# Larger load packets and smaller store packets for two of twelve slabs of a rotation kernel, and an earlier first store

## Chip, cores, metric

One core of a Trainium2 chip. The metric is the device time of one execution in microseconds (us). The kernel is bound by its DMA transfers from the second microsecond to the last.

## The reference

```python
def setup_inputs():
    batch, c, h, w = 32, 3, 256, 256
    return {"x": np.random.randn(batch, c, h, w).astype(np.float32)}

def reference(x):
    return np.rot90(x, k=-1, axes=(-2, -1)).astype(np.float32)
```

96 images of 256 x 256 floats are turned by 90 degrees: 25.17 MB in, 25.17 MB out.

## The kernel before

Twelve slabs of 8 images lie in SBUF (2.1 MB each; 4096 floats per partition). A slab comes in one of two layouts. In the *short* layout a partition holds 8 rows of each of two images, and the HBM side is runs of 8 KB; in the *long* layout it holds 16 rows of one image, runs of 16 KB. The turn on the vector engine changes one layout into the other: what is loaded short is stored long, and what is loaded long is stored short. (The two pairs 8, 9 and 10, 11 are long on both sides.) One run becomes one DMA packet, so the layout decides the packet size of the load and, the other way round, of the store.

```python
    RL, RS = 16, 8
    I = 2
    ...
    long_st = (0, 1, 2)            # loaded short, stored long
    both = (8, 10)
    ...
    for n in (0, 1, 2, 3, 7, 4, 5, 6, *range(8, n_slabs)):
        if n in (1, 2):
            nc.sync.dma_start(out=fours(units[n]), in_=ld_short[n])          # 2 MB, 8 KB packets
            continue
        for i in range(I):
            if n in long_st:
                ld = nc.sync.dma_start(out=fours(units[n])[:, i], in_=ld_short[n][:, i])
            else:
                ld = nc.sync.dma_start(out=units[n][i::I], in_=ld_long[n, i])  # 1 MB, 16 KB packets
            if (n, i) == (last, 0):
                mark = ld
    ...
    def store(n):
        if n in paired:
            first = n if n in both else n - 1
            for i in range(I):
                nc.sync.dma_start(out=st_long[n, i], in_=pairs[both.index(first)][n - first :: I, i])
        elif n in long_st:
            for i in range(I):
                nc.sync.dma_start(out=st_long[n, i], in_=home[n][i::I])
        else:
            return nc.sync.dma_start(out=st_short[n], in_=fours(home[n]))   # 2 MB, 8 KB packets

    for n in range(both[0]):
        turn(n)
    for n in (4, 3, 5, 6, 7, 1, 2):
        st = store(n)
        if n == 4:
            # the first store waits for the load called mark
            tc.add_manual_dep(st.ins, mark.ins.name, ...)
    for n in range(both[0], n_slabs):
        turn(n)
        store(n)
    ...                                # the copies of slab 0, then store(0)
```

All transfers are issued by one queue, at most eight are outstanding. Loads come first, then five stores of 8 KB packets (slabs 4, 3, 5, 6, 7), then stores of 16 KB packets.

## Time and profile before

| | |
|---|---|
| device time, median (range) of the first 3 runs | 123.25 us (123.25 to 123.33) |
| span of the profiled execution | 121.5 us |
| DMA share of the span | 97.9% |
| vector engine busy | 90.6 us (75%) |
| transfers: loads | 20 of 1 MB, 2 of 2 MB |
| transfers: stores | 14 of 1 MB, 5 of 2 MB |

The span is shorter than the device time by a constant 1.8 us or so. The lines that carry the reading are shown in the prediction. Two things help to follow the rest. A *landing* is the moment when a transfer's completion arrives; each of the 16 DMA engines reports its own, so a landing has a middle (median engine) and an end (slowest engine). And the trace records each packet with start, size and duration, but not its engine, and each engine's arrival of a completion; where I say "packet records" or "arrivals" I mean these.

### The profile page before, as it was taken

To read this page: it belongs to the slowest core of one execution; us is meant where nothing else is said; L and a number is where in the kernel's file an instruction comes from. 1 tells how busy PE (TensorE), PEld (TensorE's weight loads), DVE (VectorE), ACT (ScalarE), POOL (GpSimd) and SP (SyncE) were. 2 spreads that over 40 slices of the span, in tenths; PEclk is the share of its full clock that TensorE was granted. 3 is DMA by queue.
4 is the path that set the end of the run, shared out by engine and by line. 5 is a ranking of instruction groups with operands and counts; after the bars stand their busy time and mean duration, and the time that the engine had idled before them with its cause. 6 is when DMAs were issued, how large, how long until landed. Compare 5 with 4: busy or idle time off the path is not lost.

```text
span 121.5 us, 134 instructions
## 1 busy us (share of the span) xinstructions
DVE 90.6 (75%) x24; ACT 4.9 (4%) x3; POOL 0.2 (0%) x4
## 2 busy tenths in 40 slices
DVE  0029999999999999999999999999999960000000
ACT  0000000000000000000040000000000038000000
POOL 0000000000000000000000000000000000000000
DMA  3999999999999999999999999999999999999994
GB/s 73 426 429 426 432 458 426 426 421 421 432 432 432 421 432 432 426 426 432 432 405 426 421 429 431 432 423 431 453 432 432 432 432 432 432 432 432 432 432 173
DMA packets 4752, 50.33 MB, mean 414 GB/s; under 512 B 656, under 2 KB 656, under 8 KB 656
## 3 DMA queue, kind: packets, MB, share of 16 engines
q1 hardware_dynamic: 4752, 50.33, 97.9%
HBM read 25.17 MB, written 25.17 MB: 414 GB/s over the span
## 4 chain that ended last, share of the span: by engine, by line
DVE 59%; issue 13%; DMA 6%; DVEq 3%; ACT 2%; ACTq 1%; SPq 0%
DVE u L116 53%; DVE turned L116 6%; DMA u<-in_x_dram 6%; DVEq L169 3%; ACT u L141 2%; ACTq L169 1%; SPq L92 0%; DVEq L116 0%
## 5 line engine op out<-in xcount | busy, mean ns | idle before, releaser
L116 DVE STREAM_TRANSPOSE u<-u 128x2048 f32<-128x2048 f32 x22 | 83.5, 3866 | 0.3
L116 DVE STREAM_TRANSPOSE turned<-u 128x2048 f32<-128x2048 f32 x2 | 7.1, 3586 | 8.2 <-DMA u<-in_x_dram 8.2
L141 ACT COPY u<-turned 128x2048 f32<-128x2048 f32 x2 | 3.6, 1869 | 35.6 <-DVE u L116 35.6
L141 ACT ACT_TABLE_LOAD x1 | 1.3, 1283 | 62.2 <-DMA u<-in_x_dram 62.2
L158 POOL MEMSET const-bfloat16-1.0<- 128x1 bf16 x1 | 0.1, 101 | 0.0
L158 POOL MEMSET const-uint8-127<- 128x1 uint8 x1 | 0.1, 101 | 0.0
L158 POOL MEMSET const-float32-0.0<- 128x1 f32 x1 | 0.1, 98 | 0.2 <-issue 0.2
L158 POOL MEMSET const-float32-1.0<- 128x1 f32 x1 | 0.1, 98 | 0.0
## 6 DMA issues: line engine op xcount, KB each, us to landing
u<-in_x_dram SPq DMA_DIRECT2D x20, 1024.0 KB, 19.6
out_dram<-u SPq DMA_DIRECT2D x14, 1024.0 KB, 15.6
out_dram<-u SPq DMA_DIRECT2D x5, 2048.0 KB, 16.0
u<-in_x_dram SPq DMA_DIRECT2D x2, 2048.0 KB, 13.7
```

The source lines that it names most:

```text
L116: nc.vector.transpose(out=dst[:, h * step : (h + 1) * step], in_=src[:, h * step : (h + 1) * step])
L141: nc.scalar.copy(out=fours(units[last])[:, i], in_=fours(turned0)[:, i])
L158: nc = _bacc.Bacc("TRN2", target_bir_lowering=False, num_devices=1)
L169: with _tile.TileContext(nc) as tc:
```

## The change

Its intent: slabs 1 and 2 change layout, so that their loads use 16 KB packets, which were cheaper while loading, and their stores the 8 KB form. The last slab's first load is cut into 14 rows and 2 rows, and the first store waits for the 14 rows only. The diff also merges the two stores of slabs 8 and 10 into one transfer each.

```diff
-    long_st = (0, 1, 2)
+    long_st = (0,)
@@
-        if n in (1, 2):
+        if n in ():
             nc.sync.dma_start(out=fours(units[n]), in_=ld_short[n])
             continue
@@ the long loads
-                ld = nc.sync.dma_start(out=units[n][i::I], in_=ld_long[n, i])
-            if (n, i) == (last, 0):
-                mark = ld
+                cuts = (0, 14 * W, RL * W) if (n, i) == (last, 0) else (0, RL * W)
+                for f0, f1 in zip(cuts, cuts[1:]):
+                    ld = nc.sync.dma_start(out=units[n][i::I, f0:f1], in_=ld_long[n, i][:, f0:f1])
+                    if f1 == 14 * W:
+                        mark = ld
@@ def store(n):
         if n in paired:
             first = n if n in both else n - 1
+            if n == first:
+                nc.sync.dma_start(out=st_long[n].transpose([1, 0, 2]), in_=pairs[both.index(n)][::I])
+                return
```

## The prediction

> **What bounds the kernel now.** I read the page from the top. Slices first: is any engine, or the DMA row, full throughout?
>
> ```profile
> DVE  0029999999999999999999999999999960000000
> DMA  3999999999999999999999999999999999999994
> GB/s 73 426 429 426 432 458 426 426 421 421 432 432 432 421 432 432 426 426 432 432 405 426 421 429 431 432 423 431 453 432 432 432 432 432 432 432 432 432 432 173
> DMA packets 4752, 50.33 MB, mean 414 GB/s; under 512 B 656, under 2 KB 656, under 8 KB 656
> q1 hardware_dynamic: 4752, 50.33, 97.9%
> ```
>
> The DMA row is 9 from the second slice to the last but one, and its share of the span is 97.9%. The vector engine (DVE) is full for two thirds, then stops with 22 us to go. 50.33 MB is input plus output, so no byte can be saved: the time is a short start, one unbroken stream on 16 engines, and a short tail. 656 small packets are 41 transfers by 16 engines; the other 4096 carry data, half of 16 KB and half of 8 KB.
>
> One slice says 405, two say 458 and 453. A packet is counted whole where it starts, so I asked for the stages apart, with borders inside stretches of one kind, and for two windows of equal length around the turn from loads to stores:
>
> ```profile
> core 0: us, DVE busy (x) ACT busy (x) POOL busy (x), PEclk, DMA share, GB/s
> 20.50:59.70 39.20, 39.03 (x11) 0.00 (x0) 0.00 (x0) 1.00 1.01 429
> 66.60:86.10 19.50, 19.43 (x6) 0.00 (x0) 0.00 (x0) 1.00 1.01 429
> 88.60:118.00 29.40, 10.54 (x3) 3.63 (x2) 0.00 (x0) 1.00 1.01 429
> ...
> 54.00:59.00 5.00, 4.97 (x3) 0.00 (x0) 0.00 (x0) 1.00 1.02 433
> 59.00:64.00 5.00, 4.97 (x2) 1.28 (x1) 0.00 (x0) 1.00 0.97 411
> ```
>
> Loads of 16 KB, stores of 8 KB and stores of 16 KB run at the same 429. The window of the turn shows 0.97. Is that a real hole of 0.15 us, or counting? At its left edge 16 KB packets (0.614 us) that began earlier are lost, half a packet on average, 0.31 us; at its right edge 8 KB packets (0.310 us) give back only 0.155. The difference, 0.15 us of 5, is the 3% that is missing. A second reading confirms it: the first store is issued at 59.77 (timeline) and lands 7.3 us later, at 67.07 (the shortest of its line's landings, third row below); the scalar engine's table load, which waits for a load, is let go at 62.24, so the last load has landed by then.
>
> ```profile
> 59.77 3.29 SPq L127 DMA_DIRECT2D out_dram<-u  x4
> 62.24 1.28 ACT L141 ACT_TABLE_LOAD   x1 [62.24 <-DMA u<-in_x_dram]
> DMA to landing us min/median/max: 7.3/16.0/19.2
> ```
>
> From 62.24 to 67.07 are 4.83 us, and 2.10 MB at 429 GB/s need 4.89. There is no room for a hole. I also laid the trace's packet records side by side: the first begins at 1.77 us, the last ends at 120.30, and from 3.0 to 120.0 the 16 engines are never short of a packet. Durations of single packets and arrivals on single engines below are from these records too.
>
> **What a load of either form costs.** Eight transfers may be outstanding, so in the load stage each issue is released by the landing of the one eight earlier. The issue times are landings. The timeline of the queue, asked in narrow windows:
>
> ```profile
> 8.14 0.47 SPq L94 DMA_DIRECT2D u<-in_x_dram  x1
> 13.12 0.47 SPq L94 DMA_DIRECT2D u<-in_x_dram  x1
> 18.09 0.47 SPq L94 DMA_DIRECT2D u<-in_x_dram  x1
> ...
> 20.53 0.47 SPq L94 DMA_DIRECT2D u<-in_x_dram  x1
> 30.32 0.47 SPq L94 DMA_DIRECT2D u<-in_x_dram  x1
> ```
>
> 8.14 to 18.09 is the passage of slabs 1 and 2 in 8 KB packets: 9.95 us. 20.53 to 30.32 is four 16 KB transfers of 1 MB, the same 4.19 MB: 9.79 us.
>
> **What the Trainium skill says.** In "DMA: Bandwidth & Descriptors", section "Why small descriptors are slow (HBM only)", each packet carries a fixed overhead of about 3 cycles and 32 bytes of metadata. The trace agrees in kind: load packets average 310.0 ns for 8 KB and 614.1 ns for 16 KB, so two small ones cost 5.9 ns more than a large one, about 1%. The same page, section "Queues, rings and completion order", says that each engine consumes descriptors in ring order; so a store issued earlier waits behind the last load all the same. The trace agrees: the first store's landing is one transfer after the last load's. Section "Why a DMA increments its semaphore by 16 and not by 1" lets a transfer use 16 engines when the slowest dimension of both sides divides by 16; all new shapes begin with 64 or 128, and 656 = 41 x 16 shows 64 and 128 rows behaving so now.
>
> **The change part by part.** The instruction order of the built kernels shows what moves.
>
> Loads of slabs 1 and 2: two transfers of 2 MB in 8 KB packets become four of 1 MB in 16 KB packets. From the issue times, 9.79 instead of 9.95: -0.16 us. The packet means say 16 large packets per engine x 5.9 ns = -0.09. I take -0.14. It lies on the stream that sets the end.
>
> Stores of these slabs: four of 1 MB in 16 KB packets become two of 2 MB in 8 KB packets. The stages read 429 and 429; the packet means (309.1 against 613.6 ns) would make it 16 x 4.6 ns = 0.07 slower, the landings (4.87 us for 2 MB of 8 KB, 4.89 for two 1 MB of 16 KB) 0.04 faster. I take 0.
>
> The split load: 4 packets of 16 KB per engine become 4 of 14 KB and 4 of 2 KB, so 4 more packets at 5.9 ns, and one more completion record at 9 ns: +0.03 us.
>
> The diff has a fourth part: the first store of each pair's first slab becomes one transfer of 2 MB in place of two. Packets stay at 16 KB; two completion records per engine go: -0.02 us.
>
> The earlier release: 14 of 16 rows land 2/16 of 2.45 us, 0.31 us, before the whole transfer would. The first store is issued at 59.77 - 0.31 - 0.14, about 59.3. It lies beside other work entirely: the queue is not empty then, since the 2 rows and a load of 1 MB (2.45 us) are ahead. A hand-over needs about 1.05 us (first issue at 0.72, first packet at 1.77), and it had 61.65 - 59.77 = 1.9 us already, 61.65 being the earliest arrival of the last load on an engine. Worth 0.
>
> The vector engine: 24 transposes stay. Four take the other form; rows in the windows of either form average 3988 and 3964 ns, so the sum changes by 4 x 24 = 0.1 us at most. It is not on the path: the store that its last work for the queue releases is issued at 99.16 and lands 9.3 us later (the shortest of its line's landings); its own 1 MB takes 2.45 of these, so it stood 6.9 us behind older stores and the hand-over.
>
> Sum: -0.14 + 0 + 0.03 - 0.02 + 0 = -0.13 us. 123.25 - 0.13 = 123.12 us, and a profiled span near 121.4.
>
> **The rivals.** First, the hole at the turn is real: then the earlier store fills up to 0.15 us more, and the time is 122.97. The slice of 405 speaks for it; the arithmetic of the edges, the 4.83 us and the packet records against. Second, the odd lengths hurt: packets of 14 KB may be cut into smaller pieces, or 2 KB packets at the turn may cost more than 82 ns (5.9 plus a quarter of 304). If 14 KB went out as seven of 2 KB, 24 more packets per engine x 6 ns = 0.14, and the gain is gone: 123.26. Nothing in this profile shows such a packet, all are 8 or 16 KB. Third, the order of packets in memory matters: the stream of stores would then read slower or faster than 429 in the changed slabs or in the merged 2 MB transfers, whose packets alternate between two images. 1% of the 8.4 MB touched is 0.2 us, so 122.9 or 123.3. Against it speaks that all three kinds of stage agree to 0.3%. Fourth, the vector engine or the queue becomes the bound because eight outstanding transfers now hold 8 MB and not 10 at the start: 8 MB is 19 us of stream, against issue times of half a microsecond, so no.
>
> **Range and chances.** The three medianed runs before lie within 0.08 us, so the gain is little above the spread and far below 2% (2.5 us). No path above reaches that. I put 8 in 10 on 122.92 to 123.28: the first rival with a little noise below, the second above. Faster by over 2% one in a hundred, slower the same, for something that I don't see.
>
> **What would show it.** The issue times of the loads that wait for slabs 1 and 2 should be 2.45 us apart everywhere; the last load should land about 0.1 us sooner, near 62.1 by the table load. The first store should be issued near 59.3 and take longer to land, 7.6 us instead of 7.3: earlier issue, same landing. Packets: 4096 + 64 for the split = 4160 of data, 40 x 16 = 640 small, 4800 in all, 64 more between 2 KB and 8 KB. Store stages should stay at 429. I am wrong if the first store lands over 0.2 us earlier than the stream's shortening explains, if 14 KB appears in pieces, if the vector engine shows idle time before the last stores, or if the DMA row shows a hole.

## The result

| | before | after |
|---|---|---|
| median (range) of the timed runs | 123.25 us (123.20 to 123.62, 6 runs) | 123.81 us (123.53 to 124.07, 6 runs) |
| ratio | | 1.0041, interval 1.0023 to 1.0058 |
| span of the profiled execution | 121.5 us | 122.0 us |

A ratio is the mean time of one kernel's runs over that of the other's of the same rounds, so it is not quite the ratio of the medians. The change was to save 0.13 us and costs about 0.5 us. Within 2% the two are the same; the interval excludes 1.

The page's slices of the vector engine and of the DMA engines and its DMA part, after:

```profile
DVE  0039999999999999999999999999999940000000
DMA  3999999999999999999999999999999999999993
GB/s 89 427 435 430 430 430 430 430 430 430 430 430 430 430 430 430 430 424 430 429 406 427 430 419 424 430 430 430 416 427 424 451 430 424 424 430 419 419 430 161
DMA packets 4800, 50.33 MB, mean 413 GB/s; under 512 B 640, under 2 KB 640, under 8 KB 704
q1 hardware_dynamic: 4800, 50.33, 97.6%
```

Both rows are full where they were. The packet counts are the predicted ones: 4800, of them 640 completion records, and 64 packets of 2 KB more in the last class. The stretch of loads (slices 3 to 20) is as smooth as expected. Among the stores, behind the slice of the turn (406, the counting effect), there are slices of 416 and 419, where before had one of 421 and one of 423.

The timeline of the queue and of the scalar engine, after, and then the landings of the first seven stores from the view of their line:

```profile
8.03 0.47 SPq L96 DMA_DIRECT2D u<-in_x_dram  x1
10.47 0.47 SPq L96 DMA_DIRECT2D u<-in_x_dram  x1
12.93 0.47 SPq L96 DMA_DIRECT2D u<-in_x_dram  x1
15.37 0.47 SPq L96 DMA_DIRECT2D u<-in_x_dram  x1
...
59.20 3.40 SPq L132 DMA_DIRECT2D out_dram<-u  x4
61.95 1.28 ACT L146 ACT_TABLE_LOAD   x1 [61.95 <-DMA u<-in_x_dram]
```

```profile
DMA to landing us min/median/max: 7.6/16.6/24.8
```

Up to here everything is as predicted. The issues that show slab 1 and the first half of slab 2 landing are 2.44 to 2.46 us apart. The loads are through by 61.95 where they were by 62.24. The first store is issued at 59.20 (59.3 predicted) and takes 7.6 us instead of 7.3. The time is lost after that.

The table by stage, after, for a window of loads and one inside the first five stores:

```profile
core 0: us, DVE busy (x) ACT busy (x) POOL busy (x), PEclk, DMA share, GB/s
20.50:59.00 38.50, 38.33 (x11) 0.00 (x0) 0.00 (x0) 1.00 1.01 429
66.60:86.10 19.50, 19.43 (x6) 0.00 (x0) 0.00 (x0) 1.00 1.01 425
```

Both windows read 429 before; the stores now read 425. But GB/s in a window is a poor measure for what follows, since one packet more or less on each engine at the borders is 131 KB, nearly 7 GB/s in a window of 19.5 us. A measure without that fault is the engines' time per byte: the DMA line of a window gives packets, MB and the share of 16 engines, and share x width / MB x 16 x 8192 bytes is the time of 8 KB on one engine. The first five stores, in the window from 66.6 to 86.1 us, are touched by no part of the change but the time of the first issue. The DMA line of that window, before:

```profile
q1 hardware_dynamic: 1070, 8.37, 101.4%
```

1.014 x 19.5 / 8.37 x 131.07 = 309.6 ns. After:

```profile
q1 hardware_dynamic: 1074, 8.29, 100.9%
```

1.009 x 19.5 / 8.29 x 131.07 = 311.1 ns. (The digits allow an error of about 0.3 ns; the packet records give 309.1 and 310.5 without the completion records.) The same transfers, with the same packets, are slower after the change.

The arrivals show the whole sum. From the last load's landing to the last store's, each time on the slowest engine, before took 120.65 - 62.15 = 58.51 us (rounded from the records) and after 121.18 - 61.89 = 59.29 us, 0.78 longer. Of this 0.35 us is in the first five stores, 0.25 in the next 4.2 MB (stored as 8 KB packets now) and 0.19 in the last 10.5 MB. The gain of the loads, 0.26 us on the slowest engine, is to be taken off, and the 0.5 us of the spans are left. In this execution the median engine ends only 0.07 us later than before (120.64 against 120.57), but two engines end 0.49 and 0.54 us behind it; before, the last was 0.08 behind. The slowest engine thus shows two things at once. On the mean of the 16 engines the same stage took 58.93 us instead of 58.63, 0.30 longer, and only 0.11 of this lies in the first five stores; the rest of the 0.78 is engines drifting apart. Nor is it a matter of 8 KB packets alone: from 99 to 118 us the 16 KB store packets averaged 615.9 ns, before 614.1.

### The profile page after: what moved, and what is told of

Its sections match the earlier page's. It is cut to its first block, busy times and chain, and to the rows that moved or that the text cites. A ratio compares the mean times of both kernels' runs of the same rounds, so it can differ in the third digit from the quotient of the medians.

```text
span 122.0 us, 134 instructions
## 1 busy us (share of the span) xinstructions
DVE 90.5 (74%) x24; ACT 4.9 (4%) x3; POOL 0.2 (0%) x4
## 4 chain that ended last, share of the span: by engine, by line
DMA 51%; DVE 20%; issue 3%; DVEq 3%; SPq 3%; ACT 2%; ACTq 1%
DMA u<-in_x_dram 45%; DVE u L118 20%; DMA out_dram<-u 6%; DVEq L174 3%; SPq L96 2%; ACT u L146 2%; ACTq L174 1%; SPq L92 1%; DVEq L118 0%; SPq L132 0%
```

## The experiments

Each kernel was timed in 5 rounds against the kernel before on the same chip. "ns" is the time of 8 KB on one engine as above, in the first five stores; "stage" is the time from the last load's landing to the last store's on the slowest engine. Kernels with a wrong result are marked; they move the same bytes, but turn or store a slab whose load had the other layout.

### Which part

**The slab part alone** (slabs_only), right results.

```diff
-    long_st = (0, 1, 2)
+    long_st = (0,)
-        if n in (1, 2):
+        if n in ():
```

> The first of the parts alone: slabs 1 and 2 with 16 KB loads and 8 KB stores, nothing else. Theory A (the two extra 8 KB store transfers, whose packets alternate between two images 1 MB apart, let two engines fall behind): the cost of the whole change sits here, 123.7 to 123.9 us, and the last stores land over half a us apart between the engines. Theory B (the merged 2 MB stores of 16 KB packets do it): 123.1 us, the load saving alone. Theory C (the split load and the earlier first store change the engines' phases at the turn): 123.1 us too.

Measured: 123.93 us, ratio 1.0048 (1.0035 to 1.0061). The window of the first five stores:

```profile
q1 hardware_dynamic: 1065, 8.27, 101.2%
```

312.8 ns, and a stage of 59.49 us. The whole cost is in this part. Against theory A, the slowing is there in the first five stores and not only in the two extra ones, and about half of the engines fall behind here, not two.

**The split load alone** (split_only), right results: the hunk with `cuts` of the diff above and nothing else.

> The split of the last slab's first load and the earlier first store alone. Theory C: 123.6 us or more, engines apart by over half a us at the end. Theories A and B: 123.28 us, four more packets and a completion record per engine, the spread between engines at the end as before, about 0.2 us.

Measured: 123.27 us, ratio 1.0003 (0.9991 to 1.0015), stage 58.46 us. The first five stores:

```profile
q1 hardware_dynamic: 1072, 8.39, 101.6%
```

309.5 ns. The earlier first store (issued at 59.44) is worth nothing and costs nothing that these runs resolve.

**The merged stores alone** (merge_only), right results: the hunk `if n == first` of the diff.

> The merged store of the first slab of each pair alone (2 MB in one transfer, packets of 16 KB that alternate between two images). Theory B: 123.5 us or more, with the slowing in the last 15 us. Theories A and C: 123.23 us, two completion records per engine fewer.

Measured: 123.33 us, ratio 1.0004 (0.9992 to 1.0016), stage 58.61 us, 309.4 ns. Theories B and C fall.

**The changed kernel again** (changed_again).

> The changed kernel unaltered, on the chip of the three parts, for their sum and for the spread between executions. If the loss is in the kernel: 123.7 to 123.9 us, median engine of the last landing about 120.6 and the slowest about 0.5 us behind it. If it was the luck of one chip or one start: nearer 123.1 us.

Measured: 123.60 us (123.34 to 123.78, 6 runs), ratio 1.0025 (1.0012 to 1.0037). The profiled execution happened to be the quickest, 123.34 us, and its first five stores were undisturbed:

```profile
q1 hardware_dynamic: 1084, 8.36, 101.2%
```

309.4 ns; the first 8 KB packet longer than usual after the turn to stores came at 81.8 us. So the loss varies from one execution to the next, while the program is the same.

### Loads or stores

**The loads' form alone** (load_form_only), wrong result: slabs 1 and 2 are loaded with 16 KB packets, turned and stored as before.

```diff
-        if n in (1, 2):
+        if n in ():
-            if n in long_st:
+            if n == 0:
                 ld = nc.sync.dma_start(out=fours(units[n])[:, i], in_=ld_short[n][:, i])
```

> Wrong result on purpose: slabs 1 and 2 are loaded with 16 KB packets, but turned and stored as before, so their values land in wrong places; times and transfers stay valid. Theory L (the loads' form leaves the 16 engines in phases in which all later 8 KB stores collide): 123.6 us or more, and already the first five stores, which are the same as before, take 4.92 us and more each instead of 4.87. Theory S (the two extra 8 KB stores are what is slow): 123.05 us, the load saving of 0.19 us in full and nothing lost.

Measured: 123.84 us (123.55 to 123.88), ratio 1.0035 (1.0021 to 1.0048).

```profile
q1 hardware_dynamic: 1062, 8.31, 101.5%
```

312.2 ns; the loads end at 61.91 on the slowest engine (62.15 and 62.01 in two profiles of before), the stage is 59.16 us. The loads save what was predicted, and the *unchanged* stores then lose more than that.

**The stores' form alone** (store_form_only), wrong result: loads as before, slabs 1 and 2 stored with 8 KB packets.

```diff
-        elif n in long_st:
+        elif n == 0:
```

> Wrong result on purpose: loads as before, slabs 1 and 2 are stored with 8 KB packets. Theory S: 123.8 to 124.0 us, loss from the sixth store on. Theory L: 123.2 us, as before.

Measured: 123.50 us (123.42 to 123.68), ratio 1.0017 (1.0004 to 1.0029), stage 58.71 us.

```profile
q1 hardware_dynamic: 1080, 8.33, 101.3%
```

The two new stores take 4.96 and 4.97 us on the median engine, the five ahead of them 4.86 to 4.90. A smaller loss of its own: 0.0035 + 0.0017 is the slab part's 1.0048 within the intervals. But the line gives 310.8 ns for the first five stores, which this run leaves as they were, loads included: in this profile 167 of their 1223 packets behind the turn were longer than 309 ns, from 74.3 us on. So 18 us of 8 KB loads are no guarantee, and it isn't shown that the two new stores are slow in themselves.

**The kernel before again** (before_again).

> The kernel before, unaltered, for a second profile and the spread: 123.2 to 123.3 us with one execution in ten near 123.5; the first five stores 4.87 us each. If its profile shows stores of 4.92 us and more as well, the slowing is luck of an execution and only more frequent after the change.

Measured: 123.25 us (123.20 to 123.34), ratio 0.9996 (0.9983 to 1.0008), stage 58.55 us. In its first five stores, from 62.0 to 86.4 us, two of 1240 packets of 8 KB were longer than 309 ns.

**The slab part again** (slabs_again).

> The slab part again, for a second profile on another occasion: 123.7 to 124.0 us. If the slowing begins with the first store in every such execution, the cause lies before the stores (theory L); if it begins with the sixth, in the extra stores (theory S).

Measured: 123.69 us (123.59 to 124.01), ratio 1.0033 (1.0020 to 1.0046), stage 59.17 us. This profile caught the onset. The packet records of 16 engines, one row for each beat of 306 ns; each number is a packet's start in ns after the row's, "+15" means that it took 15 ns over 309 (a packet lasts 309 ns and the next one starts 306 ns after it, so the records overlap a little):

```
72080   2 10 20 37    75 142 149 164 167 178 195 251 254 255 263 287
72386   2 10 19 37    75 142 149 164 166 178 195 251 253 255 263 286
72692   2 10 19 37+15 75 142 149 164 166 178 195 251 253 255 263 286
72998   2 10 19 51+24 74 142 149 164 166 178 194 251 253 254 263 286
73304   1 10 19 74    74 141 148 164 166 178 194 251 253 254 263 286
73610   1 10 19 74    77 141 148 164 166 178 194 251 253 254 262 286
73916   1  9 19 74    75+3 141+2 148 164 166 178 194 251 253 254 262 286
```

Up to 72.4 us the 16 engines run in lockstep: each starts its packet at its own place in the beat, and no packet is stretched. Then one engine is held up by 15 and 24 ns and comes to lie with another at 74. From there on one or two packets in most beats are stretched, later many, and it does not heal within the 8 KB stores. In the kernel before, the lockstep lasted from the turn to 80 us and beyond in both profiles, but for a single packet; in load_form_only it was already broken in the first microsecond of stores. Neither theory's onset came: the first break was at neither the first nor the sixth store here.

### Why should loads matter that ended 40 us earlier?

**The same number and order of load transfers, but 8 KB packets** (loads_8k_1mb), right results: the first hunk of load_form_only alone, so that slabs 1 and 2 come as four transfers of 1 MB.

> Right results. Slabs 1 and 2 keep their 8 KB load packets, but come as four transfers of 1 MB, one image each, as in the 16 KB form, instead of two of 2 MB that alternate between images. Theory N (the number and order of load transfers, which shifts the queue's place and the semaphores by two, is what upsets the stores): 123.6 us or more. Theory K (the size of the load packets does): 123.27 us, two more completion records per engine, and the first five stores at 309 ns a packet without exception.

Measured: 123.44 us against 123.36 of before, ratio 0.9999 (0.9987 to 1.0012), stage 58.55 us.

```profile
q1 hardware_dynamic: 1078, 8.43, 102.2%
```

309.9 ns. Theory N falls: it is the packets of the loads, not the number or order of the transfers. With the packet size, though, the 16 KB form changes three other things: the number of packets, the partitions that a transfer fills (64 instead of 128), and the time at which the last load lands.

**The queue's place restored** (load_form_plus14), wrong result.

```diff
 (load_form_only, and)
+                cuts = (0, 14 * W, RL * W) if n in (4, 5) and i == 0 else (0, RL * W)
+                ...            # the load in the pieces of cuts
+                if n == 6:
+                    nc.sync.dma_start(out=pad[:, i, :128], in_=rows_in[16 * i : 16 * i + 16, :128])
```

> Wrong result on purpose, as the load form alone, with the queue's place restored: before its stores each engine has passed 142 descriptors in the kernel before and 128 with the load form alone; two split loads and two tiny loads add 14. Theory R (the place in the descriptor ring decides whether the 8 KB stores run undisturbed): 123.2 us and stores of 4.87 us. Theories K and N: 123.9 us, as the load form alone with 0.1 us of extra packets.

Measured: 123.70 us (123.56 to 123.92), ratio 1.0026 (1.0013 to 1.0039), stage 58.80 us, 310.5 ns, lockstep to 71.3 us. Not restored, so theory R does not hold as stated; but less disturbed than the load form alone, so the run is no clean test.

**The last load's time restored** (load_form_late), wrong result: one load of 64 KB more, into 16 partitions.

> Wrong result on purpose, as the load form alone with one load of 64 KB more (4 KB per engine, 0.16 us), so that the last load lands when it did before. Theory T (the stores start 0.17 us earlier against the vector engine's events and the later issues): 123.25 us, stores of 4.87 us. Otherwise: 124.0 us.

Measured: 124.12 us (124.02 to 124.30), ratio 1.0061 (1.0048 to 1.0074). The extra load cost far more than the 0.16 us I gave it: the last load landed at 62.30 on the median engine instead of 61.77, and the page shows a slice of 359 where the load was. A likely reason is in the Trainium skill, page "SBUF — State Buffer", section "Door 1": a range of 16 partitions reaches 4 of the 16 ports, which for 64 KB makes 0.60 us by its 109 GB/s (an estimate); I had spread it over 16 engines and forgotten the ports. The packet records fit this, but no run tests it: the sixteen packets of 4 KB took 159 to 164 ns each, as I had reckoned, and the sixteen 16 KB packets behind them took 1073 to 1280 ns instead of some 614. Its stores were nearly undisturbed (309.8 ns, stage 58.67 us), which theory T would welcome, but the turn came 0.34 us later than before, not at its time, and the stall moved the engines' starts against one another. Inconclusive.

**Slab 2's load alone** (load_form_slab2), wrong result: `if n == 1` in place of `if n in ()` in load_form_only.

> Wrong result on purpose: of the two slabs only slab 2 is loaded with 16 KB packets. Theory K: between the two, 123.4 to 123.6 us. Theories R and T leave it open, since the place (135) and the time (0.08 us earlier) are others again; a value at 123.2 us would say that the effect is no matter of dose.

Measured: 123.27 us (before: 123.36), ratio 0.9996 (0.9983 to 1.0010), stage 58.54 us, 309.5 ns. No harm.

**Slab 1's load alone** (load_form_slab1), wrong result: `if n == 2` there.

> Wrong result on purpose: of the two slabs slab 1 is loaded with 16 KB packets, slab 2 with 8 KB, so that the 8 KB loads come in two stretches. If only the number of 8 KB packets matters: as slab 2 alone, 123.2 to 123.3 us. If the first stretch must be long enough: 123.5 us and more. If the last 8 KB stretch settles the engines as well: 123.2 to 123.3 us.

Measured: 123.34 us, but from 123.10 to 124.02 in six runs; ratio 1.0015 (0.9994 to 1.0036). The profiled execution was undisturbed (309.4 ns, stage 58.59 us). Two of the six timed runs, 123.60 and 124.02, were like those of the changed kernel.

**The 8 KB loads moved to the end** (load_form_8k_end), wrong result.

```diff
 (load_form_only, and)
-            if n == 0:
+            if n in (0, 10, 11):
```

> Wrong result on purpose: slabs 1 and 2 with 16 KB packets, and in their place the last two slabs, the 10 us of load just ahead of the stores, with 8 KB packets. Same number of packets of each size as before. If an 8 KB stretch settles the engines, wherever it stands: 123.25 us, stores of 4.87 us. If what happens early in the stream is what counts (first 18 us): 123.6 us and more, with slow stores.

Measured: 123.72 us (123.66 to 123.85), ratio 1.0036 (1.0024 to 1.0048), stage 58.74 us, 310.6 ns. The 8 KB loads at the end were themselves disturbed: in the window from 52.5 to 61.5 us three packets in four were longer than 309 ns (mean 313.7), while in the kernel before, from 8.2 to 17.5 us, it was one in five (mean 310.3). So it is not a matter of stores: 8 KB packets late in the stream are disturbed in either direction, and ten microseconds of them do not settle the engines.

**No 8 KB load at all** (loads_all_16k), wrong result: `if n in ()` there.

> Wrong result on purpose: slab 0 is loaded with 16 KB packets too, no 8 KB load is left. Settling theory: the stores are disturbed from the first on, 123.7 us or more in spite of a load saving of some 0.24 us. If it is the change from 8 KB to 16 KB at 7.9 us that upsets the engines: 123.0 us.

Measured: 124.14 us (124.02 to 124.32), ratio 1.0070 (1.0058 to 1.0082).

```profile
q1 hardware_dynamic: 1060, 8.27, 101.4%
```

313.4 ns, the most disturbed of all, stage 59.17 us. Some of the loss is another: the very first load landed at 5.68 us on the median engine, where it was 5.35 to 5.48 elsewhere, and the last load 0.28 us later than in load_form_only on the slowest engine (62.19 against 61.91). The stage is as long as there (59.16), so by this measure no opening at all is no worse than 8 us of it.

**The version that keeps what did no harm** (slab2_only), right results: `long_st = (0, 1)` and `if n == 1`.

> Right results: slab 2 alone has 16 KB loads and 8 KB stores, one 8 KB store more than before and 0.08 us less loading. From the parts (slab 2's load alone 0.9996, both slabs' stores alone 1.0017, so one of them about 1.0008) 123.25 to 123.35 us: the same as before, not better. A version that beats it would show 123.15 us or less.

Measured: 123.60 us (123.30 to 123.87, 6 runs), ratio 1.0024 (1.0010 to 1.0038). Slower than expected from the parts. It does not beat the kernel before.

**A pair that differs in a discarded load only** (lead_8k and lead_16k), wrong result. Both need the same packets as load_form_only; behind slab 0 both load slabs 1 and 2 once more and throw that away, one with 8 KB packets and one with 16 KB.

```diff
 (load_form_only, and)
+        if n == 1:
+            for m in (1, 2):
+                for i in range(I):
+                    nc.sync.dma_start(out=fours(units[m])[:, i], in_=ld_short[m][:, i])    # lead_8k
+                    nc.sync.dma_start(out=units[m][i::I], in_=ld_long[m, i])               # lead_16k, in its place
```

> Wrong result on purpose (as the load form alone). Behind slab 0 the slabs 1 and 2 are loaded twice: first with 8 KB packets, which is thrown away, then with 16 KB packets as in the load form alone. 4.19 MB more, 9.95 us, so that the stream opens with 16 us of 8 KB packets although all needed packets of slabs 1 and 2 are of 16 KB. If the opening stretch protects the stores: 123.08 + 9.95 = 133.0 us, and 58.5 to 58.6 us from the last load's landing to the last store's. If not: 133.5 us and over 59.1 us.

> The same with the thrown-away load in 16 KB packets: 6 us of 8 KB packets at the start. If the opening stretch protects: disturbed stores, 123.84 + 9.79 = 133.6 us, longer than its twin though its packets are 0.16 us cheaper. If it does not: the same stores as the twin and 0.16 us less time.

Measured: 133.16 us (133.03 to 133.43), ratio 1.0804 (1.0789 to 1.0819), for the 8 KB lead; 133.29 us (133.18 to 133.51, 4 runs), ratio 1.0815 (1.0800 to 1.0830), for the 16 KB lead. The first five stores, 76.5 to 96.0 us, of the 8 KB lead and then of the 16 KB lead:

```profile
q1 hardware_dynamic: 1073, 8.40, 101.8%
```

```profile
q1 hardware_dynamic: 1064, 8.32, 101.4%
```

309.7 and 311.5 ns; stages 58.64 and 58.83 us. The loads of the 8 KB lead end 0.25 us later on the median engine (71.70 against 71.45), and it is still no slower in total. So the opening stretch protects in sign, but the two times overlap in their intervals, and the 16 KB lead was less disturbed than I expected (133.6 us).

### All together

"Opening" is the length of the unbroken stretch of 8 KB packets at the start of the loads.

| kernel | opening, us | 8 KB stores | ratio | ns, first five stores | stage, us |
|---|---|---|---|---|---|
| before_again | 18 | 5 | 0.9996 | 309.4 | 58.55 |
| loads_8k_1mb | 18 | 5 | 0.9999 | 309.9 | 58.55 |
| split_only, merge_only | 18 | 5 | 1.0003, 1.0004 | 309.5, 309.4 | 58.46, 58.61 |
| load_form_slab2 | 13 | 5 | 0.9996 | 309.5 | 58.54 |
| load_form_slab1 | 8, and 5 later | 5 | 1.0015 | 309.4 | 58.59 |
| load_form_only | 8 | 5 | 1.0035 | 312.2 | 59.16 |
| load_form_8k_end | 8, and 10 at the end | 5 | 1.0036 | 310.6 | 58.74 |
| loads_all_16k | none | 5 | 1.0070 | 313.4 | 59.17 |
| store_form_only | 18 | 7 | 1.0017 | 310.8 | 58.71 |
| slab2_only | 13 | 6 | 1.0024 | 310.9 | 59.18 |
| slabs_only, slabs_again | 8 | 7 | 1.0048, 1.0033 | 312.8, 310.3 | 59.49, 59.17 |
| after, changed_again | 8 | 7 | 1.0041, 1.0025 | 311.1, 309.4 | 59.29, 58.75 |

(The opening is counted here to the landing of its last transfer; the expectations counted from the first packet, so theirs are 2 us shorter. The ratio is of 4 to 6 timed runs; ns and stage are of one profiled execution.)

The ns column depends on when the lockstep happened to break in the one execution profiled. Take as the break the first 8 KB packet over 309 ns after 62.9 us that two more follow within 3 us. In the six profiles with slabs 1 and 2 loaded in 8 KB packets (before, before_again, loads_8k_1mb, split_only, merge_only, store_form_only), it came at 80.5 us or later, or not at all in the first five stores, but for store_form_only (74.3). In the twelve profiles with slab 1 or 2 or both loaded in 16 KB packets (the two of the lead pair left aside), it came between 63.0 and 75.9 us but for load_form_slab2 (83.1) and changed_again (81.8). Once begun it grew: in the profile of after the stretched packets rose from 5 in the 2 us from 62 us to 72 in those from 90 us, of some 104. So the break is in part chance; with the 16 KB loads it came early far more often.

**What is shown:** the slab part costs the time. The form of the loads of slabs 1 and 2 is enough to make the later stores slower, by more than the loads gain (load_form_only 1.0035 against loads_8k_1mb 0.9999); the number and order of the load transfers are not. Packet size was not parted cleanly from what changes with it: load_form_plus14 and load_form_late were meant for that and failed. The changed form of the stores costs a little by itself (1.0017). The split and the merge do nothing measurable.

**What is argued only:** that a long opening of 8 KB packets lets the engines find places in the beat that 8 KB packets can keep, and that these places persist through the 16 KB loads. The order of the ratios and the sign of the pair agree with it; store_form_only and slab2_only, which broke early behind 18 and 13 us, speak against it as a rule. The engines' arrivals keep their offsets from one another to 0.03 us through the 16 KB loads in the profile of before, but just as well in those of after and load_form_only, so this does not tell the kernels apart. Also, the records carry no engine number, so I could not see which engines disturb each other, and no run shows what they contend for. What gives the first push (such as that at 72.7 us in slabs_again) is open too.

## Why the prediction was wrong

- *What bounds the kernel* was right: the stream of packets is unbroken in every run (fewer than 15 packets under way for at most 0.14 us in all between 3 us and the last stores), the hole at the turn was a counting effect (the first rival was rightly rejected: split_only gained nothing, and though the window 59 to 64 us reads 0.94 after, the packets' time within its borders is 1.01 of the engines'), and the vector engine never came onto the path.
- *Loads of slabs 1 and 2, -0.14 us*, was right as far as it went: the last load landed 0.10 to 0.24 us earlier in load_form_only. The step that failed is the sentence that this saving "lies on the stream that sets the end" and so comes through. The sum treated the stream as a chain of packets whose times add and don't depend on one another. The load form alone came out 0.35% slower, not 0.1% faster: the stores behind gave back the saving and some 0.4 us more.
- *Stores of these slabs, 0*, was mis-sized: alone they measured +0.17%, some 0.2 us. The 4.87 us for a store of 8 KB packets was read in a stretch of the kernel before in which nothing was disturbed; the added ones, which run later, took 4.96 us, in a profile whose lockstep had broken at 74.3 us.
- *The split load, +0.03*, and *the fourth part, -0.02*, are within the noise of their runs (1.0003 and 1.0004, each within 0.12%), and *the earlier release, 0*, was right, by the mechanism given: issue at 59.2, landing 7.6 us later.
- *The third rival* was the nearest. It named stores that run slower than 429, but looked for them in the changed slabs and the merged transfers, and set them aside because all stages of the kernel before agreed to 0.3%. That agreement was a property of the kernel before, not of the packets.
- *What would show it* caught the miss: "store stages should stay at 429". But the measure named there was too coarse for 1%; the engines' time per byte shows it.
- *The range* was set by the first two rivals, with a little noise taken from the 0.08 us between three runs of the kernel before. That was too small: over the six runs of the result it spread over 0.42 us, and the changed kernel over 0.54. No rival in it made transfers slower that the change leaves alone.

## What to carry to other kernels

When a stream of transfers is saturated, a cheaper packet in one stage need not be time saved (here 0.26 us less in the loads and 0.78 us more behind them): look at the durations of the packets in the later stages as well, as share x width / MB of a window, and compare several executions. Change packet sizes in one stage at a time, and keep a run with the loads alone and one with the stores alone; here only these showed that the loss is made in transfers which the change does not touch. An earlier release was worth nothing here (1.0003), where the queue was not empty when it came.

## What the Trainium skill lacked or had wrong

- "DMA: Bandwidth & Descriptors", section "Why small descriptors are slow (HBM only)", gives a packet a fixed overhead, and no page tells of a packet time that depends on what was moved long before. In these runs an 8 KB store packet of the saturated stream took 309 ns in lockstep and 313.1 ns on average in the first five stores of loads_all_16k, with single packets tens of ns longer, and it changed with the form of loads that had ended 40 us earlier.
- The same page, section "Where 436 GB/s comes from", says that for HBM to SBUF the HBM side of about 358 GB/s binds. This core, alone, moved 414 GB/s over the whole span and 429 in its stages, so that limit did not bind; the page "HBM Reference", section "Specifications (TRN2)", has it right with about 425 for a core that streams alone.
- "SBUF — State Buffer", section "Door 1", gives rates for a narrow range of partitions, but not where a trace shows the cost: in load_form_late the 64 KB load's own packets took 159 to 164 ns, and the packets behind it took 1073 to 1280 ns, for 0.53 us in all.
